# A decoder layer on one core: the sums of w_down in the first gate/up phase move from VectorE to GpSimd, and their stores to GpSimd's queue

## The chip, the cores and the metric

The kernel runs on one core of one Trainium2 chip. The metric is the device time of one execution in microseconds (us); the time before is the median of three runs. The core has TensorE (PE, matrix products), VectorE (DVE), ScalarE (ACT) and GpSimd (POOL) for work element by element, and SyncE (SP), whose queue issues most of the transfers between the chip's memory and the on-chip buffers. Each engine takes its own instructions strictly in order.

## The reference

One decoder layer over 2048 tokens of width 1024, in float32. A first half mixes tokens: sliding-window attention in one group of channels, a causal depthwise convolution of width 31 in the other, and an output projection. The second half is the feed-forward part with which this case deals:

```python
hn = rms_norm(h, ffn_pre_g)
ff = (jax.nn.silu(hn @ w_gate) * (hn @ w_up)) @ w_down
h = h + rms_norm(ff, ffn_post_g)
```

`w_gate` and `w_up` are 1024 x 2816, `w_down` is 2816 x 1024.

## The kernel before

**Products.** Each float32 operand is split into a rounded part and the remainder, and a product is three TensorE passes (high by high, high by low, low by high). The splits run on ScalarE (`split_f`, line 782, and line 133) and VectorE or GpSimd (`lo`, line 786).

**Seven products instead of eight.** The feed-forward products are done on 2 x 2 blocks with seven block products, so both operands are first combined by sums and differences. For gate and up, `stage_p1` (line 942) makes four sums per weight pair on VectorE (line 961 on); for down, four differences of each 2 x 2 block of `w_down` are needed. These are the same for all tokens, so they are computed once, by `stage_tsums` (line 1065), and stored to a DRAM tensor `td`, from which `stage_p2` (line 1103) loads them in both of its runs.

**Stages.** Tokens go in four tiles of 512. First come projections, attention and output projection of all tiles (labels A, B, W), with the convolution's taps (`fc@C`, VectorE) as background work. Then, for token tiles 0 and 1: `stage_pre`, `stage_p1` (label F: gate and up), `stage_p2` (label G: down); then the same for tiles 2 and 3. What this document calls the first gate/up phase is the first run of `stage_p1`; `stage_tsums` runs beside it, and so do taps of a later tile.

**What sets the order.** The program is written as generators. A main generator yields the time that a step should take (2.76 per block product in `stage_p1`); after each step `run` (line 1339) gives every `Lane` credit in proportion to its rate, and lanes emit work while they have credit. `stage_tsums` is alone in lane `lt` (rate 0.3): it loads four blocks, costs 3, and then costs 1 per difference. A scheduler then sets the final order on each engine from the data dependences and priorities. Taps are tied by `dve` (line 83) to the newest VectorE instruction of the main stream so that they keep pace with it; `ptt` (line 103) is GpSimd's plain `tensor_tensor` and has no such tie.

**Buffers.** `stage_tsums` holds its four blocks in one `wx` tile (two blocks; one buffer in all, line 53) and two `fc` tiles (three buffers in all, shared with the taps' accumulators). The differences are made in place, so the next set of loads has to wait until the stores of this set have landed:

```python
b11, b12, b21, b22 = b
for to, o, p_, q_ in ((0, b11, b12, b11), (2, b12, b22, b12), (1, b22, b22, b11), (3, b21, b21, b22)):
```

**Names in the profile.** `wx@G<-w_down`, `fc@G<-w_down` (line 1072): the loads of `stage_tsums`, from SyncE's queue. `wx@G`, `fc@G` on VectorE: the differences (VectorE's instructions all carry line 85, the helper `dve`). `td<-wx@G`, `td<-fc@G` (line 1078): the stores. Of the gate/up phase: `raw@F`, `chl@F`: weights and their sums, loaded at lines 956 and 958; `w@F`: split weights; `mm@F`: product banks; `gb@F` and `at@F`: partial products, which VectorE adds to a bank that it reads (line 1035); `gb@F<-keeps` (line 988): loads of products that `stage_pre` made, which ScalarE copies into a bank (line 1017); `mids`: where the gated products go; `y_scr`: where finished taps go (line 570).

Of the kernel before, what the change touches and what calls it, by code (L numbers as in the profile page):

```python
# [18 lines left out]
ALU = mybir.AluOpType  # L19
# [18 lines left out]
def layer_kernel(ctx, tc, x, xT, cols, rows, sinks, relb, onehot, w_in, w_pw, w_out, w_gate, w_up, w_down, out):  # L38
    nc = tc.nc
# [18 lines left out]
    def f4(tag, shape=(P, D)):  # L58
        return t_(tag, shape)

    def f2(tag, shape=(P, T)):
        return t_(tag, shape)
# [20 lines left out]
    def dve(op):  # L83
        def emit(*args, **kw):
            r = op(*args, **kw)  # L85
            if not paced[0]:
                pace["main"] = r.ins
            elif pace["main"] is not None and pace["main"] is not pace["tied"]:
                tc.add_manual_dep(
                    r.ins,  # L90
                    pace["main"].name,
                    mybir.DependencyInfo(mybir.DependencyClass.NoSync, mybir.DependencyReason.DATA),
                    reason="conv taps keep pace with the projections",
                )
                pace["tied"] = pace["main"]
            return r

        return emit

    stt = dve(nc.vector.scalar_tensor_tensor)  # L100
    vtt = dve(nc.vector.tensor_tensor)
    vts = dve(nc.vector.tensor_scalar)
    ptt = nc.gpsimd.tensor_tensor
# [9 lines left out]
    def tied(r):  # L113
        if lead_pe[0] is not None and lead_pe[0] is not r:
            after_first(lead_pe[0], r)
        return r
# [948 lines left out]
    def stage_tsums(td):  # L1065
        L = "G0"
        for pr in range(NF // 2):
            lab[0] = L
            wx = f4("wx", (P, 2, T))
            b = [wx[:, 0], wx[:, 1], f2("fc"), f2("fc")]  # L1070
            for i, (f, n) in enumerate(((0, 0), (0, 1), (1, 0), (1, 1))):
                tied(nc.sync.dma_start(b[i], w_down[2 * pr + f, :, n * T : (n + 1) * T]))
            yield 3
            b11, b12, b21, b22 = b
            for to, o, p_, q_ in ((0, b11, b12, b11), (2, b12, b22, b12), (1, b22, b22, b11), (3, b21, b21, b22)):
                lab[0] = L
                vtt(o, p_, q_, ALU.subtract)
                nc.sync.dma_start(td[to, pr], o)
                yield 1

    def finish(L, gb, jobs, pool=True):
# [317 lines left out]
    td = dr.tile([4, NF // 2, P, T], F32, name="td")  # L1399
# [7 lines left out]
    lh.add("S0", stage_h_sums(ws, ops), lambda: f"P0.{PRE_S0}" in started and "B3" in lb.done)  # L1407
    run(stage_pre(ws, ops, mids[0], keeps[0], Q0))
    lt.add("TS", stage_tsums(td))
    run(stage_p1(ws, ops, mids[0], keeps[0]))  # L1410
    lt.until("TS")
# [79 lines left out]
```

## Time and profile before

| | |
|---|---|
| median of three runs | 2038.7 us (2031.3 to 2039.29) |
| the profiled execution | 2035.91 us, of which span 2034.2 us |
| TensorE busy | 1960.4 us (96%) |
| VectorE busy | 1504.4 us (74%) |
| ScalarE busy | 986.4 us (48%) |
| GpSimd busy | 402.8 us (20%) |
| mean granted TensorE clock | 0.987 |

The profile is of one execution. Times in it count from the start of the span. A line of groups reads: line, engine, operation, output<-inputs, shapes, count | busy us, mean ns of one | idle time of the engine just before them, and what ended it. In the view of waits the columns are: total us, times, longest. A line of the timeline gives start, duration, engine, operation, and in brackets the engine's idle time before it and what ended that.

### The profile page before, as it was taken

The numbers are of one execution on the slowest core, as the hardware profiler recorded it, in microseconds if no ns is written. First come the engines' busy times: TensorE is split into PE (matmuls) and PEld (weight loads), VectorE is DVE, ScalarE is ACT, GpSimd is POOL, SyncE is SP. The second block draws the span as 40 slices with busy tenths as digits, with TensorE's granted clock in tenths as the row PEclk, the third lists the DMA queues.
The fourth block names the chain that finished last, engine by engine and source line by source line (L and its number), as shares of the span: only waits on it lengthen the run. The fifth ranks groups of instructions, "written<-read, shape, count | busy, mean of one in ns | idle before, by whom it ended". The sixth has DMA issues, their size and how long they took to land. (4 is left out here: it accounts for less than half of the span.)

```text
span 2034.2 us, 27180 instructions
## 1 busy us (share of the span) xinstructions
PE 1960.4 (96%) x8826; PEld 1566.7 (77%) x8826; DVE 1504.4 (74%) x2649; ACT 986.4 (48%) x1938; POOL 402.8 (20%) x462
## 2 busy tenths in 40 slices
PE   8999999998989999999989999999999999999998
PEld 6877767776667778788878878877788888888886
DVE  5999886994795889888649985577566665545557
ACT  5455445456546633333346457556643333345443
POOL 6011224433111300000001012115423233220000
PEclk9999999999999999999999999999999999999999
DMA  8787645578558876777376778579954443266654
GB/s 309 257 300 232 204 135 186 182 233 275 174 179 313 293 240 225 263 247 251 139 264 211 234 261 283 193 278 305 335 182 159 149 174 114 95 232 227 193 186 166
DMA packets 234110, 451.44 MB, mean 222 GB/s; under 512 B 23496, under 2 KB 49264, under 8 KB 233968
## 3 DMA queue, kind: packets, MB, share of 16 engines
q1 hardware_dynamic: 211184, 411.96, 60.9%
q10 hardware_dynamic: 20544, 30.42, 4.1%
q0 software_dynamic: 2240, 7.34, 0.9%
q8 instruction: 69, 1.13, 0.2%
q14 instruction: 73, 0.60, 0.1%
HBM read 330.60 MB, written 119.02 MB: 221 GB/s over the span
## 5 line engine op out<-in xcount | busy, mean ns | idle before, releaser
L85 DVE SCALAR_TENSOR_TENSOR fc@C<-glu@C,colt,fc@C 128x512 f32<-128x512 f32 x480 | 373.3, 791 | 3.0
L108 PE MATMUL mm@F<-hl@H,w@F 128*128 128x512 f32 x1056 | 252.4, 390 | 2.7 <-ACT mm@F L909 2.5
L108 PE MATMUL mm@G<-hl@G,hl@G 128*128 128x512 f32 x924 | 228.8, 397 | 7.0 <-DVE x@G L85 4.6
L108 PEld LDWEIGHTS mm@F<-hl@H,w@F 128*128 128x128 f32 x1056 | 197.8, 188 | 44.6 <-ACT mm@F L909 3.6
L108 PEld LDWEIGHTS mm@G<-hl@G,hl@G 128*128 128x128 f32 x924 | 173.7, 190 | 46.2 <-ACT hl@G L782 6.3
L108 PE MATMUL mm@A<-hl@A,w@A 128*128 128x512 f32 x840 | 206.6, 397 | 2.4 <-ACT hl@A L318 1.4
L782 ACT ACTIVATE w@F<-chl@F 128x512 fp32r<-128x512 f32 x220 | 135.4, 625 | 141.6 <-PE mm@F L108 134.8
L108 PE MATMUL mm@G<-w@G,hl@G 128*128 128x512 f32 x876 | 199.5, 389 | 0.0
L108 PEld LDWEIGHTS mm@G<-w@G,hl@G 128*128 128x128 f32 x876 | 164.5, 188 | 34.1
L108 PEld LDWEIGHTS mm@A<-hl@A,w@A 128*128 128x128 f32 x840 | 156.0, 189 | 38.0 <-DVE hl@A L85 2.3
L85 DVE TENSOR_TENSOR w@F<-chl@F,w@F 128x512 fp32r<-128x512 f32 x198 | 144.6, 732 | 35.8 <-ACT w@F L782 35.4
L108 PE MATMUL mm@F<-ql@H,w@F 128*128 128x512 f32 x528 | 128.5, 391 | 4.8 <-ACT w@F L782 3.1
L108 PE MATMUL mm@F<-mid@H,w@F 128*128 128x512 f32 x528 | 130.6, 392 | 2.3 <-ACT mm@F L909 2.2
L108 PE MATMUL mm@F<-p@H,w@F 128*128 128x512 f32 x528 | 131.5, 395 | 0.3 <-ACT at@F L1031 0.3
L108 PE MATMUL mm@F<-x@H,w@F 128*128 128x512 f32 x528 | 126.9, 394 | 2.3 <-ACT fa@F L931 2.3
L108 PEld LDWEIGHTS mm@F<-ql@H,w@F 128*128 128x128 f32 x528 | 98.9, 188 | 27.0 <-ACT w@F L782 3.8
L108 PEld LDWEIGHTS mm@F<-x@H,w@F 128*128 128x128 f32 x528 | 100.0, 190 | 23.9 <-ACT fa@F L931 2.8
L108 PEld LDWEIGHTS mm@F<-mid@H,w@F 128*128 128x128 f32 x528 | 98.9, 189 | 25.1 <-ACT mm@F L909 3.7
L108 PEld LDWEIGHTS mm@F<-p@H,w@F 128*128 128x128 f32 x528 | 100.7, 191 | 22.1 <-ACT at@F L1031 0.9
L133 ACT ACTIVATE w@A<-raw@A 128x512 fp32r<-128x512 f32 x110 | 67.6, 627 | 94.0 <-PE mm@A L108 54.8
L108 PE MATMUL mm@W<-w@W,hl@W 128*128 128x512 f32 x384 | 100.8, 406 | 9.2 <-ACT hl@W L704 5.9
L108 PE MATMUL tr@W<-w@W,ql@W 128*128 128x512 f32 x384 | 98.7, 396 | 5.6 <-ACT mid@W L675 4.6
(302 smaller groups left out, 3385.7 us busy)
## 6 DMA issues: line engine op xcount, KB each, us to landing
mids<-fa@F SPq DMA_DIRECT2D x154, 256.0 KB, 2.6
raw@A<-w_in SPq DMA_DIRECT2D x55, 512.0 KB, 4.5
w@A<-lo_in SPq DMA_DIRECT2D x84, 256.0 KB, 3.4
fc@G<-mids SPq DMA_DIRECT2D x77, 256.0 KB, 3.4
fa@G<-mids SPq DMA_DIRECT2D x75, 256.0 KB, 4.5
gb@F<-keeps SPq DMA_DIRECT2D x72, 256.0 KB, 4.3
raw@W<-w_out SPq DMA_DIRECT2D x32, 512.0 KB, 5.5
w@W<-lo_out SPq DMA_DIRECT2D x48, 256.0 KB, 3.7
```

Source lines behind the costliest of these rows:

```text
L85: r = op(*args, **kw)
L108: r = nc.tensor.matmul(*args, **kw)
L133: act(w[:, 0], raw, AF.Copy)
L782: act(w[:, 0], x, AF.Copy)
```

## The change

In `stage_tsums`, the 44 differences (four for each of 11 pairs) are issued to GpSimd instead of VectorE, and the 44 stores of 256 KB come from GpSimd's queue instead of SyncE's. The loads of `w_down` stay in SyncE's queue. Since `ptt` carries no tie for the taps, the scheduler also orders some taps and sums of the gate/up phase a little differently.

```diff
             for to, o, p_, q_ in ((0, b11, b12, b11), (2, b12, b22, b12), (1, b22, b22, b11), (3, b21, b21, b22)):
                 lab[0] = L
-                vtt(o, p_, q_, ALU.subtract)
-                nc.sync.dma_start(td[to, pr], o)
+                ptt(o, p_, q_, ALU.subtract)
+                nc.gpsimd.dma_start(td[to, pr], o)
                 yield 1
```

## The prediction

> **What bounds the kernel now.** I read the page first: the line of busy times and POOL's row of the 40 slices.
>
> ```profile
> span 2034.2 us, 27180 instructions
> PE 1960.4 (96%) x8826; PEld 1566.7 (77%) x8826; DVE 1504.4 (74%) x2649; ACT 986.4 (48%) x1938; POOL 402.8 (20%) x462
> ...
> POOL 6011224433111300000001012115423233220000
> ```
>
> TensorE is busy for 96% of the span, so moving work between other engines can only win what TensorE loses to waits and to a lowered clock. The loads of w_down are issued from 707.6 to 932.9 us, so the stage to look at is 700 to 950 us, in which POOL has nothing to do (its slices are 0). The view of stretches, and the view of waits over the same stretch, price that stage:
>
> ```profile
> core 0: us, PE busy (x) PEld busy (x) DVE busy (x) ACT busy (x) POOL busy (x), PEclk, DMA share, GB/s
> 700.00:950.00 250.00, 242.31 (x1042) 197.84 (x1042) 216.40 (x349) 92.45 (x166) 0.00 (x0) 0.98 0.75 250
> 728.70:732.10 3.40, 3.40 (x8) 2.72 (x9) 3.40 (x6) 2.14 (x4) 0.00 (x0) 0.51 0.81 258
> 834.60:841.40 6.80, 5.95 (x14) 4.70 (x15) 5.75 (x10) 2.32 (x5) 0.00 (x0) 0.50 0.46 165
> 1500.00:1850.00 350.00, 350.00 (x1546) 289.91 (x1545) 211.39 (x277) 138.23 (x244) 99.27 (x70) 1.00 0.47 162
> ```
> ```profile
> PE mm@F L108 <- DVE gb@F L85: 3.9, 2, 3.6
> PE mm@F L108 <- ACT w@F L782: 3.1, 1, 3.1
> PE mm@F L108 <- ACT at@F L1031: 0.3, 1, 0.3
> PE mm@F L108 <- ACT mm@F L1017: 0.2, 1, 0.2
> ```
>
> TensorE idles 250 - 242.3 = 7.7 us here, nearly all in two stalls, 3.6 and 3.1 us. After the first it runs 3.4 us at clock 0.51, after the second 6.8 us at 0.50; half of that is lost, 1.7 + 3.4 = 5.1 us. So the whole stage has 7.7 + 5.1 = **12.8 us** to give; its mean clock of 0.98 (2% of 250 us) says the same of the 5.1. Nothing more can come out of this stage, however much VectorE sheds.
>
> Both stalls come from the sums that are moved. The first, in order of time:
>
> ```profile
> 727.36 0.69 DVE L85 TENSOR_TENSOR wx@G<-wx@G 128x512 f32<-128x512 f32 x1 [2.28 <-DMA wx@G<-w_down]
> 727.97 0.68 DVE L85 TENSOR_TENSOR gb@F<-gb@F,mm@F 128x512 f32<-128x512 f32 x1
> 728.71 2.90 PE L108 MATMUL mm@F<-yt@H,w@F 128*128 128x512 f32 x6 [3.60 <-DVE gb@F L85]
> ```
>
> VectorE stands 2.28 us at a w_down sum whose load has not landed. Behind it in the same queue is the read of a product bank (gb@F), for which TensorE waits 3.60 us. The second stall:
>
> ```profile
> 824.05 3.00 SPq L1078 DMA_DIRECT2D td<-wx@G  x2
> 826.00 0.69 DVE L85 TENSOR_TENSOR wx@G<-fc@G,wx@G 128x512 f32<-128x512 f32 x1 [1.92 <-DMA fc@G<-w_down]
> 828.89 0.42 SPq L988 DMA_DIRECT2D gb@F<-keeps  x1
> 834.25 0.60 ACT L1017 ACTIVATE mm@F<-gb@F 128x512 f32<-128x512 f32 x1 [8.80 <-DMA gb@F<-keeps]
> 835.45 1.22 PE L108 MATMUL mm@F<-ql@H,w@F 128*128 128x512 f32 x2 [3.06 <-ACT w@F L782]
> ```
>
> VectorE stands 1.92 us at a sum, SyncE's queue is held by the store of that sum (two stores over 3.00 us), and behind it the load of gb@F goes out late; ScalarE waits 8.80 us for gb@F, and the weight split behind that wait stops TensorE for 3.06 us.
>
> **The change part by part.** *Removed from VectorE:* four sums for each of 11 pairs.
>
> ```profile
> L85 DVE TENSOR_TENSOR wx@G<-wx@G 128x512 f32<-128x512 f32 x11 | 7.6, 690 | 7.5 <-DMA wx@G<-w_down 6.7 <-DMA fc@G<-w_down 0.8
> L85 DVE TENSOR_TENSOR wx@G<-fc@G,wx@G 128x512 f32<-128x512 f32 x11 | 7.6, 688 | 4.6 <-DMA fc@G<-w_down 4.5
> L85 DVE TENSOR_TENSOR fc@G<-fc@G,fc@G 128x512 f32<-128x512 f32 x11 | 7.5, 683 | 0.0
> L85 DVE TENSOR_TENSOR fc@G<-fc@G,wx@G 128x512 f32<-128x512 f32 x11 | 7.5, 683 | 0.0
> ```
>
> 7.6 + 7.6 + 7.5 + 7.5 = 30.2 us of work, and 7.5 + 4.6 = 12.1 us of waits that stand ahead of them in VectorE's queue.
>
> *Added to POOL:* the same 44 sums, with POOL reading and writing SBUF beside a VectorE that is 216.4/250 = 87% busy. A POOL operation of this size took 99.27/70 = 1.42 us in the second gate/up stage (1500 to 1850 us, above), so 44 x 1.42 = 62 us. The issue of a store takes POOL 0.56 us:
>
> ```profile
> L137 POOL DMA_DIRECT2D lo_out<-w@W x16 | 8.9, 557 | 2.1 <-POOL w@W L135 2.1
> ```
>
> 44 of them make 25 us. Together that is 87 us in some 230 us of an idle engine: POOL itself bounds nothing. But there VectorE pays for POOL's work. Rows of that stretch, then the first and the last of these groups in 700 to 950 us:
>
> ```profile
> L85 DVE TENSOR_TENSOR w@F<-chl@F,w@F 128x512 fp32r<-128x512 f32 x79 | 62.6, 795 | 29.1 <-ACT w@F L782 28.8
> L85 DVE TENSOR_TENSOR chl@F<-raw@F,chl@F 128x512 f32<-128x512 f32 x38 | 32.5, 895 | 0.7
> L85 DVE TENSOR_TENSOR fa@F<-fa@F,gb@F 128x512 f32<-128x512 f32 x11 | 17.2, 1567 | 0.0
> ```
> ```profile
> L85 DVE TENSOR_TENSOR w@F<-chl@F,w@F 128x512 fp32r<-128x512 f32 x87 | 59.2, 683 | 1.5 <-ACT w@F L782 1.4
> L85 DVE TENSOR_TENSOR fa@F<-fa@F,gb@F 128x512 f32<-128x512 f32 x8 | 5.5, 683 | 0.0
> ```
>
> Against 0.683 us without POOL, the three groups took 79 x 0.112 + 38 x 0.212 + 11 x 0.884 = 26.6 us longer, 0.38 us for each of the 70 POOL operations, at a VectorE 211/350 = 60% busy; the last group took 0.88 us longer. At 87% busy I scale 0.38 to 0.55 as the lower bound, and the upper is the whole POOL operation, 1.42. I take 0.7, between 0.55 and 0.88 where the rows lie: 44 x 0.7 = 31 us. So VectorE's work stays the same (-30 + 31), in smaller pieces: its gain is the 12.1 us of waits alone.
>
> The Trainium skill, "SBUF — State Buffer", section "Who interferes with whom", says that a VectorE instruction with two SBUF inputs contends with a GpSimd instruction that reads SBUF, and that the one which comes second blocks fully. The rows agree in kind (0.683 against 1.567); taken to its end it gives a result of its own, the second rival below.
>
> *Moved from SyncE's queue to POOL's:* 44 stores. What they cost SyncE is mostly waiting:
>
> ```profile
> SPq L1078 <- DVE wx@G L85: 27.2, 19, 3.7
> ```
> ```profile
> L1078 SPq DMA_DIRECT2D td<-fc@G x22: 319/320/425, 720.2 to 945.1; - x22
> ```
>
> Some 27 us of waits for the sums into wx go, and 44 x 0.32 = 14 us of issuing. The stores themselves land later:
>
> ```profile
> td<-wx@G SPq DMA_DIRECT2D x22, 256.0 KB, 2.7
> wx@G<-w_down SPq DMA_DIRECT2D x22, 256.0 KB, 4.8
> lo_in<-w@A POOLq DMA_DIRECT2D x12, 256.0 KB, 5.6
> lo_out<-w@W POOLq DMA_DIRECT2D x16, 256.0 KB, 4.8
> ```
>
> 2.7 us from SyncE, 4.8 to 5.6 us from POOL. By the built order of instructions POOL does sum, store, sum, store in turn, and nothing else stands in its queue until the stage ends.
>
> *Added wait.* There is one wx buffer, so the next set's loads, which stay in SyncE's queue, wait for POOL's stores; behind them are the loads of chl@F and of gb@F, of which the latter made the second stall. A set turns round in 4.8 (load) + 4 x 1.42 + 4 x 0.56 + 5.2 (store) = 17.9 us, for the wx buffer alone in 4.8 + 3 x 1.42 + 2 x 0.56 + 5.2 = 15.4 us. The sets now start like this:
>
> ```profile
> 707.55 0.93 SPq L1072 DMA_DIRECT2D wx@G<-w_down  x2
> 721.82 0.85 SPq L1072 DMA_DIRECT2D wx@G<-w_down  x2
> 737.19 0.84 SPq L1072 DMA_DIRECT2D wx@G<-w_down  x2
> ```
> ```profile
> L1072 SPq DMA_DIRECT2D wx@G<-w_down x22: 333/424/508, 707.6 to 932.9; - x22
> ```
>
> 14.3 and 15.4 us for the first three, but (932.9 - 707.6)/10 = 22.5 us on average. So SyncE is held by 1 to 4 us at the second and third set, right where TensorE would be 5 us ahead by the first stall's removal; later sets have room.
>
> *The sum.* First stall: 3.6 + 1.7 = 5.3 us, bounds 0 and 5.3. The wait at 727.36 is gone for certain, but what is late next is the third set's hold on SyncE; I keep 3.0. Second stall: 3.1 + 3.4 = 6.5 us. Without the 1.92 us wait and the store that holds SyncE, gb@F goes out at least 1.9 us earlier, so 3.1 falls to about 1.2 and is probably too short for the lowered clock (the waits of 0.2 and 0.3 us above cost none): bounds 1.9 and 6.5, I take 5.0. The small waits: 7.7 - 3.6 - 3.1 = 1.0 us, I take 0.5. Against it, VectorE's longer operations ahead of a bank read, 0.5 (0 to 3, one POOL operation twice). 3.0 + 5.0 + 0.5 - 0.5 = **8.0 us faster**. The profiled execution took 2035.9 us (span 2034.2 and 1.7 around it), so 2027.9; that execution is 2.8 us under the median of the three runs, 2038.7, which themselves lie from 2031.3 to 2039.3. With the terms at their bounds the forecast reaches from 2023.1 (all 12.8) to 2037.
>
> **The rivals.** *An exchange.* POOL's turn-round takes VectorE's place: SyncE stands at the w_down loads of the second, third and a later close pair of sets, gb@F and chl@F come as late as now, and the stalls appear elsewhere. For it: ScalarE already waits 8.8 us at the worst gb@F, and a hold of 4 us is of that size. Against it: the mean distance of the sets, 22.5 us, is longer than the turn-round of 17.9. Only the second stall's 1.9 us are kept: 2034, within 2030 and 2041.
>
> *VectorE becomes the bound (slower).* If each POOL operation blocks VectorE for its whole length, 44 x 1.42 = 62.5 us come for 30.2: VectorE is busy 216.4 + 32.3 = 248.7 us, and with the 250 - 216.4 - 12.1 = 21.5 us of its other waits the stage takes 270 us: 20 us longer, 2056. It decides from (237.2 - 186.2)/44 = 1.16 us per operation if those other waits give way, or 0.67 if none does (237.2 = the stage without stalls, 186.2 = VectorE without the sums). For it: 0.88 in the last group. Against it: that group's is the worst row, and in 1500 to 1850 us, at 70 POOL operations, TensorE is busy 350.0 of 350 us. The Trainium skill's "Perfetto Trace Analysis", section "Optimizing Scalar/DVE Operations", warns that moving work between these two engines might not help; by that the result lies between this rival and the exchange.
>
> That the change does not do what it says is excluded: in the built order all 44 sums and stores stand in POOL's queue.
>
> **How the numbers follow.** Forecast 0.50 (2028), exchange 0.35 (2034), VectorE as bound 0.15 (2056). The measurement tells about 0.5% from no change: 10.2 us, so faster is under 2028.5 and slower over 2048.9 against the median. The forecast lies at that edge: 0.35 of its 0.50 is under it, with 0.03 of the exchange; of the last rival 0.13, and 0.01 of the exchange, is over. Faster 0.38, same 0.48, slower 0.14. The range: 2023.1 less the 4.6 us by which the fastest run lies under the profiled one, 2019; up, over the exchange's end and into the last rival until 0.13 is left above, 2045.
>
> **What would show it.** Right: POOL busy about 62 us in this stage, VectorE's busy time there within 6 us of 216, no wait of VectorE for w_down, no half clock after 728 and 835 us, waits of SyncE at L1072 for td of 1 to 4 us in the first sets. Wrong: VectorE's busy time over 235 us there (the port), new waits of ScalarE at L1017 over 8 us behind L1072 (the turn-round), or the stage shorter while a later one takes the time back.

## The result, and the profile after

The changed kernel took **2062.5 us** (median of 6 runs, 2060.7 to 2071.1) against 2038.2 us before (6 runs, 2031.3 to 2039.8): ratio 1.013, 95% interval 1.011 to 1.015. It is 24 us slower; the forecast was 2028 us. The profiled execution took 2060.7 us. Its page, first part and POOL's row of the slices:

```profile
span 2059.0 us, 27216 instructions
...
PE 1966.6 (96%) x8826; PEld 1566.1 (76%) x8826; DVE 1526.7 (74%) x2605; ACT 986.1 (48%) x1938; POOL 486.5 (24%) x550
...
POOL 6011133442111332322001103106423333220000
```

VectorE has 44 instructions less (2605 for 2649) and is busy 22 us longer. Its remaining instructions became longer. The stage from 700 to 950 us in the view of stretches (columns as before: PE, PEld, DVE, ACT, POOL, clock, share and rate of the transfers), and what TensorE waits for in it:

```profile
700.00:950.00 250.00, 227.47 (x953) 181.95 (x952) 221.81 (x280) 85.27 (x154) 76.85 (x80) 0.97 0.67 228
```
```profile
PE mm@F L108 <- DVE gb@F L85: 8.5, 5, 3.0
PE mm@F L108 <- DVE fa@F L85: 8.1, 4, 5.3
PE mm@F L108 <- DVE w@F L85: 3.8, 1, 3.8
PE mm@F L108 <- ACT w@F L782: 2.0, 3, 1.2
```

TensorE gets through 953 products in the time in which it did 1042, and stands 22.5 us where it stood 7.7. Three of the four waits are for VectorE itself. VectorE is busy 221.8 us, only 5 more than before, but for 280 operations in place of 349: 0.79 us each in place of 0.62. The groups (mean ns in the last column before the idle time) say which ones grew. Two rows of before come first (the third, `w@F`, stands in the prediction), then the rows after:

```profile
L85 DVE TENSOR_TENSOR chl@F<-raw@F,chl@F 128x512 f32<-128x512 f32 x35 | 23.0, 684 | 0.1
...
L85 DVE TENSOR_TENSOR gb@F<-gb@F,mm@F 128x512 f32<-128x512 f32 x16 | 10.9, 681 | 4.0 <-PE mm@F L108 4.0
```
```profile
L85 DVE TENSOR_TENSOR w@F<-chl@F,w@F 128x512 fp32r<-128x512 f32 x79 | 70.0, 889 | 0.8 <-ACT w@F L782 0.8
...
L85 DVE TENSOR_TENSOR chl@F<-raw@F,chl@F 128x512 f32<-128x512 f32 x32 | 32.5, 1054 | 0.2
...
L1077 POOL TENSOR_TENSOR wx@G<-wx@G 128x512 f32<-128x512 f32 x10 | 14.4, 1436 | 164.3 <-DMA wx@G<-w_down 164.3
...
L1077 POOL TENSOR_TENSOR fc@G<-fc@G,fc@G 128x512 f32<-128x512 f32 x10 | 13.0, 1300 | 0.2
L1078 POOL DMA_DIRECT2D td<-wx@G x20 | 11.2, 559 | 5.6 <-POOL wx@G L1077 5.6
...
L85 DVE TENSOR_TENSOR gb@F<-gb@F,mm@F 128x512 f32<-128x512 f32 x15 | 10.2, 678 | 1.4 <-PE mm@F L108 1.3
```

Operations that read two on-chip tiles went from 683 to 889 ns and from 684 to 1054; those that read one tile and one product bank (`gb@F<-gb@F,mm@F`) stayed at 678 (681 before). GpSimd itself has 164 us of idle time in front of its first sum of a pair, waiting for loads: its speed bounds nothing. The timeline at one pair shows the mechanism (a row joins neighbouring operations of one kind; x2 is two of them):

```profile
736.09 0.56 POOL L1078 DMA_DIRECT2D td<-wx@G  x1 [0.30 <-POOL wx@G L1077]
...
736.26 4.46 DVE L85 TENSOR_TENSOR chl@F<-raw@F,chl@F 128x512 f32<-128x512 f32 x2
736.67 1.31 POOL L1077 TENSOR_TENSOR fc@G<-fc@G,wx@G 128x512 f32<-128x512 f32 x1
...
738.27 0.56 POOL L1078 DMA_DIRECT2D td<-fc@G  x1 [0.30 <-POOL fc@G L1077]
...
738.85 1.31 POOL L1077 TENSOR_TENSOR fc@G<-fc@G,fc@G 128x512 f32<-128x512 f32 x1
...
740.64 0.74 DVE L85 SCALAR_TENSOR_TENSOR fc@C<-glu@C,colt,fc@C 128x512 f32<-128x512 f32 x1
```

Two VectorE operations that take 1.37 us without GpSimd take 4.46 (recorded at 736.26 for 2.27 and at 738.46 for 2.26). Each began while GpSimd still issued a store, stood through the rest of the issue and the whole sum behind it, and ended some 0.55 us after the sum. SyncE's queue shows the consequence, one line before the change and two after it:

```profile
SPq L956 <- DVE chl@F L85: 18.0, 14, 3.2
```
```profile
SPq L956 <- DVE chl@F L85: 79.6, 14, 11.1
...
SPq L1072 <- DMA y_scr<-fc@C: 1.7, 1, 1.7
```

Line 956, the load of the next weights, waits 79.6 us for VectorE to free `chl@F` (18.0 before). No wait at line 1072, the loads of w_down, is for `td`.

Over all records of the stage I added up, for each VectorE operation of 128x512 on two on-chip tiles that overlaps a sum on GpSimd, its duration over 0.684 us (0.744 for a tap): **48.8 us for 44 sums, 1.11 us each**. Off VectorE went 30.2 us. This sum, called the block below, is used for every run.

### The profile page after: what moved, and what is told of

It is laid out like the page before. It is cut to its first block, busy times and chain, and to the rows that moved or that the text cites. A ratio compares the mean times of both kernels' runs of the same rounds, so it can differ in the third digit from the quotient of the medians.

```text
span 2059.0 us, 27216 instructions
## 1 busy us (share of the span) xinstructions
PE 1966.6 (96%) x8826; PEld 1566.1 (76%) x8826; DVE 1526.7 (74%) x2605; ACT 986.1 (48%) x1938; POOL 486.5 (24%) x550
## 5 line engine op out<-in xcount | busy, mean ns | idle before, releaser
L85 DVE SCALAR_TENSOR_TENSOR fc@C<-glu@C,colt,fc@C 128x512 f32<-128x512 f32 x480 | 379.4, 804 | 3.1
L85 DVE TENSOR_TENSOR w@F<-chl@F,w@F 128x512 fp32r<-128x512 f32 x198 | 161.0, 817 | 33.4 <-ACT w@F L782 33.1
L108 PE MATMUL mm@F<-mid@H,w@F 128*128 128x512 f32 x528 | 135.4, 403 | 14.8 <-DVE fa@F L85 9.8
L499 POOL TENSOR_SCALAR_AFFINE_SELECT p@B<-p@B 128x512 f32<-128x512 f32 x62 | 55.8, 909 | 211.5 <-ACT p@B L497 210.1
```

The source lines that it names most:

```text
L108: r = nc.tensor.matmul(*args, **kw)
L499: nc.gpsimd.affine_select(out=pg[:, kb].rearrange("p (i q) -> p i q", q=P), in_=pg[:, 1].rearrange("p (i q) -> p i q", q=P), compare_op=AL ...
```

## The experiments

Four theories stood at the start. PORT: a sum on GpSimd, which reads two tiles, blocks VectorE's operations that read two tiles, and this block is the loss. QUEUE: the stores in GpSimd's queue are. ORDER: the changed order on VectorE is. And a part of the loss may come in a later stage. The first four runs take the change apart; the median of the kernel before beside them was 2037.2 us.

**Sums alone on GpSimd**, stores on SyncE:

```diff
-                nc.gpsimd.dma_start(td[to, pr], o)
+                nc.sync.dma_start(td[to, pr], o)
```

> Only the sums move to GpSimd; their stores stay in SyncE's queue. Theory PORT (VectorE's operations with two SBUF inputs stand still while GpSimd reads SBUF for a sum): the loss stays, 2052 to 2068 us, and VectorE's w@F splits in the stage stay near 870 ns. Rival QUEUE (stores from GpSimd's queue turn the wx buffer round late and hold SyncE's loads): the loss goes, 2042 us or less. Rival ORDER (without the tie the scheduler puts taps and sums in a worse order on VectorE): the loss stays, as in PORT.

Measured: 2044.8 us, ratio 1.0037 (1.0021 to 1.0053): under a third of the loss, which no theory had. The block is 37.1 us, 0.84 per sum, 6.9 over the 30.2 removed. That this is near the loss of 7.5 us is chance: in the profiled execution the first product of the next stage (`mm@G`) starts only 3.4 us later than before (25.0 later in the changed kernel), and the rest of the loss lies behind that point. Such a rest of 1.4 to 6.5 us is there in the profile of every run below, whether its stage became longer or shorter, though the edits leave the work behind the stage as it is. All are measured against one execution of the kernel before, so it stays open what part of the rest is the kernels' own.

**Stores alone from GpSimd**, sums on VectorE:

```diff
-                ptt(o, p_, q_, ALU.subtract)
+                vtt(o, p_, q_, ALU.subtract)
```

> Only the stores move to GpSimd's queue; the sums stay on VectorE. PORT: no loss, 2026 to 2040 us, VectorE's splits at 683 ns. QUEUE: the loss stays, 2050 us or more. ORDER: no loss (VectorE's order is nearly that of before), 2030 to 2040.

Measured: 2037.1 us, ratio 0.9994 (0.9977 to 1.0010): no change. QUEUE falls as a cause by itself. But 0.37 and -0.06 per cent do not make 1.31: sums and stores together cost more than each alone.

**GpSimd writes but does not read:**

```diff
-                ptt(o, p_, q_, ALU.subtract)
+                for _ in range(3):
+                    nc.gpsimd.memset(o, 0.0)
```

> In place of each sum GpSimd fills the tile with zeros three times (it writes SBUF and reads nothing), and stores it; so the w_down sums are left out of the computation. VectorE's order is nearly that of the changed kernel. PORT (by reads): VectorE's operations keep their 683 ns, 2020 to 2034 us. QUEUE and ORDER: the loss stays, 2050 us or more. If GpSimd's writes block VectorE as its reads do: 2050 us or more with splits near 850 ns.

**No sums at all**, only loads and stores:

```diff
-                ptt(o, p_, q_, ALU.subtract)
```

> Neither engine computes the sums: the loaded blocks are stored as they are, from GpSimd's queue; so the w_down sums are left out of the computation. PORT: the whole of the stage's 12.8 us comes back, 2020 to 2030 us. QUEUE and ORDER: the loss stays, 2050 us or more.

Both leave the sums out of the computation. Measured, a single run each: 2033.0 and 2033.0 us. The groups of 700 to 985 us, with stores alone, then with the memsets:

```profile
L85 DVE TENSOR_TENSOR w@F<-chl@F,w@F 128x512 fp32r<-128x512 f32 x102 | 69.7, 686 | 1.6 <-ACT w@F L782 1.6
```
```profile
L85 DVE TENSOR_TENSOR w@F<-chl@F,w@F 128x512 fp32r<-128x512 f32 x102 | 69.6, 687 | 5.5 <-ACT w@F L782 5.4
...
L1078 POOL MEMSET fc@G<- 128x512 f32 x66 | 34.0, 541 | 4.6 <-DMA fc@G<-w_down 4.5
L1078 POOL MEMSET wx@G<- 128x512 f32 x66 | 33.6, 527 | 161.0 <-DMA wx@G<-w_down 160.3
```

132 memsets keep GpSimd about as busy as the sums did (67.6 us; the sums 59.8) and leave VectorE's operations at 687 ns. So here the GpSimd that only writes does not block VectorE, and the one that reads does. The Trainium skill's page "SBUF — State Buffer", section "Who interferes with whom", says just that (two inputs on VectorE against a GpSimd instruction that reads, not one that only writes), and the trace agrees. Without the sums the program takes some 4 us less than the median beside it. These are single executions; 19 of the kernel before lay between 2034.6 and 2045.7 us beside them, and others reach 2031.3. So about 4 us is the most that the runs suggest could be won by taking the sums off VectorE, whoever makes them.

ORDER falls with these two runs. Of VectorE's 2605 operations other than these sums, 66 stand at other places in the order of the changed kernel than in that of the kernel before. The run without sums differs by 20 from the changed kernel (61 from before) and the run with memsets by 32 (67 from before): they have nearly the changed order and take 2033 us, where ORDER expected 2050 or more. With sums alone on GpSimd 22 differ from the changed kernel, so the order hardly explains what these two differ by either.

**Why do stores make a sum dearer?** In the changed kernel, the 29 sums that begin within 0.5 us behind a store's issue block VectorE for 1.33 us on average and take 1.30 us themselves; the other 15 block 0.69. With sums alone on GpSimd it is 0.84 behind another sum. The same place in that run:

```profile
744.62 0.69 DVE L85 TENSOR_TENSOR w@F<-chl@F,w@F 128x512 fp32r<-128x512 f32 x1
744.88 1.58 POOL L1077 TENSOR_TENSOR wx@G<-wx@G 128x512 f32<-128x512 f32 x1 [9.57 <-DMA fc@G<-w_down]
...
745.22 1.79 DVE L85 SCALAR_TENSOR_TENSOR fc@C<-glu@C,colt,fc@C 128x512 f32<-128x512 f32 x1
...
746.53 1.61 POOL L1077 TENSOR_TENSOR wx@G<-fc@G,wx@G 128x512 f32<-128x512 f32 x1
...
746.93 1.77 DVE L85 TENSOR_TENSOR fa@F<-fa@F,at@F 128x512 f32<-128x512 f32 x1
```

Here the two engines take turns. The operation at 744.62 finishes in 0.69 and the sum takes 1.58, since it waits some 0.27 us for it; then VectorE's next waits for the sum. Behind an issue the sum hardly waits and VectorE's operation does. Four runs asked what about the issue does this, whether fewer sums cost less, and whether VectorE can win the 4 us itself (median before beside them: 2036.9 us).

*A memset in place of the issue*, stores on SyncE (EARLY against ISSUE):

```diff
                 ptt(o, p_, q_, ALU.subtract)
-                nc.gpsimd.dma_start(td[to, pr], o)
+                nc.gpsimd.memset(o, 0.0)
+                nc.sync.dma_start(td[to, pr], o)
```

> GpSimd makes the sums, SyncE stores them, and in the place where the changed kernel issues a store on GpSimd there stands a GpSimd memset of the same 128x512 tile (so the stored values are zeros, and the output is not the reference's; the order of sums and instructions between them on GpSimd is that of the changed kernel). In the changed kernel a sum that begins within 0.5 us behind a store's issue lengthens VectorE's work by 1.32 us (30 of them), in the run with sums alone on GpSimd a sum lengthens it by 0.84. Theory EARLY (a sum next in GpSimd's queue already keeps VectorE's two-input operations out while the instruction ahead of it, whatever it is, still runs): 1.15 to 1.35 us per sum, 48 to 58 us lost, GpSimd's mean sum 1.3 to 1.4, time 2053 to 2064 us. Rival ISSUE (the store's issue itself does it, by what it writes for the transfer): the memset does nothing, 0.75 to 0.95 us per sum, mean sum 1.55 to 1.6, time 2041 to 2048 us.

Measured: 2051.2 us, ratio 1.0066 (1.0044 to 1.0088). The block, 0.75 us per sum (0.79 right behind a memset), is ISSUE's; the time lies between the two ranges.

*The four issues behind the four sums* (a dependence on the last sum holds them back):

```diff
-                ptt(o, p_, q_, ALU.subtract)
-                nc.gpsimd.dma_start(td[to, pr], o)
+                last = ptt(o, p_, q_, ALU.subtract)
                 yield 1
+            for to, o in ((0, b11), (2, b12), (1, b22), (3, b21)):
+                r = nc.gpsimd.dma_start(td[to, pr], o)
+                # ordered behind last
```

> As the changed kernel, but the four stores of a pair of rows are issued on GpSimd behind all four sums, not between them. EARLY: 33 of 44 sums have a sum just ahead of them as in the run with sums alone, the stores have no sum behind them; 0.8 to 0.95 us per sum, 35 to 42 us lost, time 2042 to 2050 us. Rival BURST (the loss comes from the number of instructions that GpSimd runs in a stretch, wherever the issues stand): as the changed kernel, 1.05 to 1.2 us per sum, 2055 to 2064 us.

Measured: 2060.8 us, ratio 1.0121 (1.0103 to 1.0140). The block is 0.81 us per sum, as expected without an issue ahead, and yet the time is that of the changed kernel, as BURST had it. So the sum of the blocks alone does not set the time. That does not show BURST, because this kernel brings a wait that the changed kernel has not: with its stores issued late, SyncE stands at the load of the third set until they have landed, 9.1 us at once (690 to 985 us):

```profile
SPq L1072 <- DMA td<-wx@G: 11.3, 2, 9.1
```

Behind that load stand the loads of the next weights. The order on VectorE also differs from the changed kernel's, by 34 operations. What part of the loss is due to each was not tried.

*Half the sums:*

```diff
-                ptt(o, p_, q_, ALU.subtract)
+                (ptt if to in (0, 1) else vtt)(o, p_, q_, ALU.subtract)
```

> Two of the four sums of a pair of rows on GpSimd, the other two on VectorE, all four stores issued on GpSimd. By VectorE's balance: 22 sums that each lengthen VectorE's work by 0.85 to 1.3 us, less 22 x 0.687 = 15.1 us taken off it: +4 to +13 us in the stage, time 2040 to 2050 us. Rival THRESHOLD (VectorE has some 30 us of slack in the stage, so that half the dose costs nothing): 2033 to 2039 us.

Measured: 2051.1 us, ratio 1.0062 (1.0038 to 1.0086): about half the loss, a little over the expected end. THRESHOLD is wrong at this half: 22 sums are not free.

*Sums on VectorE, later:*

```diff
-            yield 3
+            yield 6
...
-    RT = 0.3
+    RT = 0.45
```

> The sums stay on VectorE and their stores on SyncE; only the place where the program puts them is later (6 units in place of 3 behind the loads, and a rate of 0.45 for this side work to get through in the same time). If the gain that the change was meant for lies in the waits at the head of a queue (a sum that waits for its load, a store that waits for a sum), this takes it without GpSimd: the run without sums ends 4 us earlier, so 2031 to 2036 us. Rival: the work only waits at other places, 2037 to 2043 us.

Measured: 2038.0 us, ratio 0.9998 (0.9985 to 1.0012): no gain.

**Are sums cheaper apart?** Each sum is made to wait for the TensorE instruction at its place; the second run also puts the stores on SyncE (before beside them: 2039.1 us).

```diff
-                ptt(o, p_, q_, ALU.subtract)
+                r = ptt(o, p_, q_, ALU.subtract)
+                tc.add_manual_dep(r.ins, lead_pe[0].ins.name,
+                    mybir.DependencyInfo(mybir.DependencyClass.Sync, mybir.DependencyReason.DATA), ...)
```

> As the changed kernel (sums on GpSimd, stores issued from GpSimd), but 34 of the 44 sums wait, besides for their data, for the TensorE instruction at which the program puts them, so that the four sums of a pair of rows no longer run in one stretch but some 3 us apart. Before it: with sums alone on GpSimd VectorE lost 37.1 us to them and got 30.2 off, with stores behind the four sums 35.8, with half the sums 18.0 less 15.1, yet these kernels lost 4, 16 and 10 us within the stage: TensorE stands 1 to 4 us at a time in the stretches where four sums of GpSimd run one after the other. Theory BURST (what costs is that VectorE is held back for several operations in a row, longer than what it works ahead): spread sums block one operation each, 0.6 to 0.9 us per sum, TensorE's idle time within 690 to 985 us falls from 26.7 us to below 14, time 2033 to 2044 us. Rival TOTAL (each sum costs the same wherever it runs): idle time above 20 us, 2050 to 2064 us.

> The same with the stores issued from SyncE. BURST: as the run above within 4 us, so 2033 to 2044 us. A rival, QUEUE (a store on SyncE that waits for a sum that waits for TensorE holds SyncE's loads of the weights): 2046 to 2060 us, with SyncE's waits at the store's line above 90 us within 690 to 960 us (53 us in the run with sums alone).

Measured: 2051.9 us, ratio 1.0068 (1.0049 to 1.0087), and 2051.4 us, ratio 1.0068 (1.0042 to 1.0094). TensorE's idle time from 690 to 985 us is 18.0 and 21.5 us (26.7 in the changed kernel, 7.7 before). The stores' queue makes no difference (QUEUE needed over 90 us of SyncE's waits at the store's line; there are 33). Half the loss goes; but the spreading is only half done too, 22 and 19 of the 44 sums still start within 0.5 us of the sum or issue before them. BURST's numbers were not reached: it is at most a part. The blocks of the two are 45.6 and 36.8 us, and yet their times are equal; here, too, the sum of the blocks alone does not set the time. (The second run's order on VectorE lies further from the changed kernel's, by 63 operations against 33, which may hide a gain.)

**Where in the stage?** The first five pairs and the last six apart, each with the other pairs' sums on VectorE (before beside them: 2036.7 us). In the trace before, VectorE has least room at the first pairs.

```diff
-                ptt(o, p_, q_, ALU.subtract)
+                (ptt if pr < 5 else vtt)(o, p_, q_, ALU.subtract)
```

> Pairs 0 to 4 (the first 20 sums, to about 815 us) as in the changed kernel, pairs 5 to 10 with their sums on VectorE; all stores issued from GpSimd. In the trace before, VectorE is busy 93 to 96 per cent from 730 to 790 us and 84 to 85 per cent from 850 us on. Theory DENSE (a sum's block becomes lost time where VectorE has no idle time to take it up): the changed kernel's loss to 806 us, 12 to 13 us, comes whole, less what the second half of the stage gives back (3 us in the run with stores alone): stage 8 to 13 us later, time 2045 to 2052 us. Rival PROPORTIONAL (each sum with its store costs the same, 24.4 us / 44): 11 us, 2046 to 2051 us, the same here; the next run tells.

The second run has `pr >= 5`, the third also `nc.sync` for the stores of these pairs:

> The other half: pairs 0 to 4 on VectorE, pairs 5 to 10 (24 sums) on GpSimd as in the changed kernel, all stores from GpSimd. DENSE: VectorE has 15 per cent idle time there, so at most 4 us of loss: 2034 to 2042 us. PROPORTIONAL: 24/44 of 24.4 us, 13 us: 2047 to 2054 us.

> As the run above with the stores of pairs 5 to 10 from SyncE, so that no issue of a store stands ahead of a sum on GpSimd (0.8 to 0.85 us per sum in place of 1.1 to 1.3). DENSE: no loss or a small gain (the run with sums alone on GpSimd won 3.6 us between 806 and 962 us): 2032 to 2039 us. PROPORTIONAL: 24/44 of 7.5 us, 4 us: 2040 to 2044 us.

Measured: 2047.0 us, ratio 1.0044 (1.0032 to 1.0055); 2052.5 us, ratio 1.0068 (1.0051 to 1.0084); 2043.2 us, ratio 1.0030 (1.0017 to 1.0043). The two halves, 0.44 and 0.68 per cent, add up to 1.12, near the 1.31 of the whole. DENSE is wrong for the last six pairs, with their stores on either queue (2052.5 against at most 2042, 2043.2 against at most 2039); PROPORTIONAL's ranges hold all three. Two stretches of each kernel: before, changed, first five, last six, last six with stores on SyncE. The second column is TensorE's busy time and, in brackets, its products:

```profile
690.00:810.00 120.00, 115.69 (x500) 94.29 (x499) 104.29 (x169) 45.59 (x82) 0.00 (x0) 0.99 0.72 239
810.00:985.00 175.00, 171.63 (x742) 140.83 (x742) 147.28 (x237) 66.81 (x121) 0.00 (x0) 0.98 0.76 253
```
```profile
690.00:810.00 120.00, 107.40 (x453) 86.73 (x452) 105.91 (x140) 41.66 (x75) 33.47 (x35) 0.96 0.69 235
810.00:985.00 175.00, 160.93 (x669) 128.03 (x668) 149.44 (x191) 59.81 (x108) 50.81 (x54) 0.96 0.66 226
```
```profile
690.00:810.00 120.00, 107.66 (x453) 86.94 (x452) 107.12 (x144) 42.38 (x76) 32.85 (x32) 0.96 0.67 231
810.00:985.00 175.00, 173.19 (x757) 142.91 (x757) 151.05 (x237) 66.35 (x119) 20.38 (x32) 0.99 0.73 253
```
```profile
690.00:810.00 120.00, 115.25 (x495) 93.14 (x494) 104.24 (x169) 45.12 (x82) 9.23 (x17) 0.99 0.71 242
810.00:985.00 175.00, 163.64 (x684) 132.05 (x683) 149.63 (x195) 60.17 (x111) 47.49 (x51) 0.96 0.67 234
```
```profile
690.00:810.00 120.00, 114.26 (x490) 92.19 (x489) 103.62 (x169) 44.37 (x80) 8.68 (x16) 0.99 0.71 241
810.00:985.00 175.00, 171.74 (x750) 139.91 (x749) 151.63 (x216) 66.30 (x120) 40.10 (x28) 1.00 0.73 254
```

Before, a product takes 120/500 = 0.24 us of the first stretch and 175/742 = 0.236 of the second. The changed kernel is 47 products behind in the first (11 us) and 73 in the second (17 us); 28 us by this count, while its next stage begins 25 us late. With the first five pairs alone it is 47 behind and then gains 15; with the last six, 5 and 58 behind (1 and 14 us). So within the stage the loss stands where the sums stand. The last two kernels differ in the last six pairs by the queue of the stores alone: 66 products, 16 us in this stretch, go with the 24 issues being on GpSimd. The block there is 28.4 us against 18.3, with 24 x 0.687 = 16.5 us taken off VectorE in both: a net of +11.9 and +1.8, for a stretch that comes out 14 us later and 2 us earlier. There the time goes the way of VectorE's balance, but more steeply: 10.1 us of block between the two kernels stand beside 16 us of stretch. The whole programs differ by 9 us.

In the first stretch the time does not follow the balance. There 20 sums take 20 x 0.687 = 13.7 us off VectorE. The blocks are 22.5 us in the changed kernel, 21.4 with the first five pairs alone, 16.5 with grouped issues, 16.0 with the memsets and 15.0 with sums alone: nets of 8.8, 7.7, 2.8, 2.3 and 1.3 us. The products behind (453, 453, 449, 450 and 472 done of 500) make 11, 11, 12, 12 and 7 us. What the kernels have in common is where the time goes: TensorE stands for about 1 to 6 us at a time beside the first three pairs (714 to 760 us), and its mean granted clock from 750 to 770 us is 0.83 (0.91 in the grouped kernel), where it was 1.00 before. In the changed kernel:

```profile
750.00:770.00 20.00, 14.66 (x57) 11.65 (x56) 19.55 (x27) 6.06 (x11) 5.71 (x6) 0.83 0.63 222
```

In these 20 us of the changed kernel TensorE did 57 products; 5.3 us it stood, and the mean granted clock was 0.83.

**A place and a queue of their own for VectorE's sums:** later, as above, with the stores on GpSimd.

> No sum on GpSimd: the sums on VectorE at the later places of the run before (6 units in place of 3 behind the loads), the stores from GpSimd. That run and the one with stores alone each ended level with the kernel before. If the two waits they remove (VectorE's for a load, SyncE's for a sum) are worth something together: 2030 to 2035 us; if what they win in the stage is given back behind it as in both: 2036 to 2040 us.

Measured: 2035.3 us, ratio 0.9990 (0.9979 to 1.0001): not to be told from the kernel before. None of the versions that compute the whole layer beats it measurably.

## Why the prediction was wrong

- **The step that failed** is "I take 0.7 ... So VectorE's work stays the same (-30 + 31)", and with it the term of the sum for VectorE's longer operations, "0.5 (0 to 3, one POOL operation twice)". A sum cost VectorE 1.11 us, so it stood at +18.6 us, and TensorE waited 20.4 us for VectorE in the stage (8.5 + 8.1 + 3.8), where it had waited 3.9. The 0.7 was scaled from a stretch with 0.38 per GpSimd operation by how busy VectorE is there. The range from 0.55 to 0.88 held for sums without issues ahead of them (0.84, 0.81, 0.76 in three runs); that each issue right ahead of a sum raises its price to 1.3 was missed. The prediction priced the 44 issues as GpSimd's own time alone. A right price would not have been enough: the grouped kernel has 0.81 per sum, 5.5 us over the 30.2, and is as slow as the changed one. So VectorE's total is not all that decides; where the blocks fall may count, and in the grouped kernel SyncE's wait for its stores. The two stalls that the sum priced at 3.0 and 5.0 us are gone from their places, and longer ones stand at others.
- **The rival "VectorE becomes the bound"** (2056, chance 0.15) came nearest in kind: three of TensorE's four waits are for VectorE. Its sum did not come: VectorE got +18.6 us in place of +32.3, and the time passed 2056 all the same. The prediction's own condition for it was 0.67 to 1.16 us per operation; the 0.7 taken already lay over the lower end, so the chance was set low by its own working. In the stage TensorE stands 14.8 us longer (22.5 against 7.7), and it is busy at half clock for 14.2 us (in stretches from 718.9, 753.0, 821.3 and 916.8 us) in place of 9.4, of which half is lost: 2.4 us more. Together that is 17 of the some 21 us that its 89 missing products make at 0.24 us each; the rest is not accounted for. The rival's argument against, that TensorE is busy 350 of 350 us with 70 GpSimd operations beside it, held for a VectorE at 60% and says nothing of one at 87%.
- **The 8 us to be won** are near what the stage had to give, but not by this change: the run without sums ends that stage 7 to 8 us earlier (the last load of line 956 there is issued at 954.5 us in place of 962.6). It ends the program only 4 us earlier: TensorE's wait for `x@G` (at 1349 us before) grew from 4.6 to 6.1 us, and TensorE stands 24.5 us from 985 to 1500 us where it stood 20.6. The prediction named a later stage that takes time back only as a sign. But behind the stage the runs that lost time in it are longer by as much (4.8 us with the memsets in place of issues, 6.5 with sums alone; 4.2 here), so it is not shown that a gain is taken back.
- **"Landing later" was wrong:** GpSimd's stores landed in 2.9 and 2.4 us, not 4.8 to 5.6:

```profile
td<-wx@G POOLq DMA_DIRECT2D x22, 256.0 KB, 2.9
td<-fc@G POOLq DMA_DIRECT2D x22, 256.0 KB, 2.4
```

  The rows I took were of other stages. So the turn-round, and the exchange built on it, did not come: SyncE never waited at line 1072 for `td` in this stage. (It did in the grouped kernel, 9.1 us.)
- **A sign was badly chosen.** "VectorE's busy time within 6 us of 216" came true (221.8) in a kernel 24 us slower. A fixed stretch of a stage that has become longer holds less work. Counted per product of TensorE, VectorE went from 216.4/1042 = 0.208 to 221.8/953 = 0.233 us, 12% up, which was the sign to ask for. GpSimd's 62 us for 44 sums were 59.8 (mean 1.36).
- **Right** were: GpSimd itself bounds nothing, no wait of VectorE for w_down is left, the half clock behind 728 and 835 us is gone from these places, and operations that read a product bank kept their 0.68 us.

What stays open: why an issue right ahead of a sum lets the sum go first, where a memset there does not; why the first five pairs lose 11 to 12 us even in kernels whose net block is 2 to 3 us, and why the run with sums alone on GpSimd loses less there (7 us); what part of the grouped kernel's loss is SyncE's wait for its stores; and what the 1.4 to 6.5 us behind the stage are, which every experiment's profile shows and the changed kernel's does not (-0.2 us).

## What to carry to other kernels

Moving an element-by-element operation with two on-chip inputs from a busy VectorE to GpSimd did not free VectorE here: it paid for each one somewhat more than it saved (0.75 to 0.84 us for 0.69), and far more (1.3) if a store was issued from GpSimd just ahead of it. Try the stores of GpSimd's results on another queue (2044.8 us in place of 2062.5 for all pairs, though nothing where the sums were spread), or give GpSimd work that only writes. Before costing such a move, run the kernel without the work: here two single executions of that kind put what could be won at about 4 us of 2037.

## What the runs showed of the hardware

- A store's issue on GpSimd (0.54 to 0.56 us) by itself costs VectorE nothing: 67 VectorE operations overlapping an issue in the run with stores alone were 0.00 us longer on average. In the changed kernel the 23 operations that overlap an issue and the sum right behind it were 1.48 us longer on average; the 17 that overlap an issue and a sum otherwise, 0.87.
- Right behind an issue a sum takes 1.30 us on average (changed kernel), behind another sum 1.57 (sums alone), behind a memset 1.49. The Trainium skill's page "SBUF — State Buffer", section "Who interferes with whom", says that issue order decides who is blocked; here an operation of VectorE that the trace shows starting 0.4 us ahead of the sum was still the one that waited.
- In the changed kernel TensorE's granted clock was 0.50 for 3.4 us from 718.9 us on, behind a wait of 3.8 us, and for 6.8 us from 753.0 us on, during and behind a wait of 5.3 us; the mean from 750 to 770 us was 0.83. So these waits cost more than themselves. A wait of 2.9 us that ended at 744.1 us was followed by no such stretch, another of 2.9 us that ended at 916.4 was.
